# Both halves of eight FFN chunks as seven block products, with half of the down-projection between their steps

## Chip, cores, metric

One NeuronCore of a Trainium2 chip. The metric is the device time of one execution in microseconds.

## What is computed

A trunk of two decoder layers over 512 tokens of width 1024. Layer 0 mixes tokens by dilated attention, layer 1 by a gated linear recurrence (RG-LRU); after each mixer comes the same gated ConvFFN, which is where the change lies. Every sub-layer stands between two RMS norms, and the second norm's output is added to the residual stream.

```python
D_MODEL, SEQ, D_FF, FFN_CONV_WIDTH = 1024, 512, 3 * 1024, 3

def conv_ffn(x, w_up, conv_w, conv_b, w_down):       # w_up (1024, 6144), w_down (3072, 1024)
    u = causal_dwconv(x @ w_up, conv_w, conv_b)      # depthwise, 3 taps along the tokens
    g, v = u[..., :D_FF], u[..., D_FF:]
    return (jax.nn.gelu(g, approximate=True) * v) @ w_down
...
for layer in range(DEPTH):                           # 2 layers
...
    h = rms_norm(x, norm_ffn_pre[layer])
    h = conv_ffn(h, ffn_w_up[layer], ffn_conv_w[layer], ffn_conv_b[layer], ffn_w_down[layer])
    x = x + rms_norm(h, norm_ffn_post[layer])
```

All inputs are float32.

## The kernel before

**Numbers.** Every operand of a matmul is split into a high and a low part: `split` copies the raw values to fp32r on ACT (line 147), and VectorE subtracts that copy from the raw values (line 148). A product takes three matmuls (`PASSES`: high x high, high x low, low x high). Weights go through the same split, so each weight tile that TensorE uses costs one ACT copy and one VectorE subtraction of 128 x 512.

**Weights.** All weight loads stand in one list, `plan`, in the order of use. `load` fetches the next raw chunk (1 MB) on SP's queue into one of three buffers; `pump` converts the next piece of a chunk into one of 16 pairs of high and low buffers (`HALVES`, counted in `state["live"]`). `done` gives buffers back, `take` returns a converted piece. `tick` is called after each unit of TensorE's work and lets pending side work (`sides`) and the pump run, so conversions are issued some units ahead of their use. Every engine works through its instructions in the order in which the program gives them out.

**The FFN.** `hT` holds the normed tokens transposed, features on the partitions. The 3072 gelu features and the 3072 value features are cut into 12 chunks of 256 each, and a chunk into two tiles of 128 features by 512 tokens. A plain tile is 8 x 3 matmuls of 512 columns into one PSUM bank (`feat_tile`, or in four parts `quarters`). `begin` then does the convolution (line 749 on ACT, line 753 twice on VectorE) and returns the gelu (line 765, ACT) or the multiplication of gelu and value (the gate, line 767, VectorE).

For chunks 3 to 10 (`SEVEN`) the gelu half is made by a scheme of seven block products: the 256 features, the 1024 inputs and the 512 tokens are each cut in two, and seven products of combined blocks replace eight. The token-side sums come from `token_sums`, which runs as side work while the plain chunks 1 and 2 are computed and, before the change, goes on into the stage. The weight-side sums are made in the raw buffer by `stream`: VectorE additions (lines 198 and 202), and accumulating loads issued by POOL (`add_rows`, line 184), which add a block of the same weights from DRAM to the block that lies there. A step of a product is 12 matmuls of 256 columns (line 934).

`seven` writes out the order by hand as slots. Each period of `CYCLE` = 15 slots has the seven steps of one gelu chunk (`AT` gives their slots; step 4 falls into the next period) and eight quarters of plain value tiles as fillers (6 matmuls of 512 columns each, line 392). What must follow a step is registered with `later`, which gives it out a slot later. In the stage, one piece is pumped after each slot.

After the stage come what is left of chunk 10, chunk 11 and the down-projection (`rows_proj`, `rows_run`): 24 rows of 128 features, each with 1024 output columns in two halves, summed in eight PSUM banks (`acc`), two for each of the four tiles of 128 tokens. `act_split` splits the gated activations one row at a time. The order of passes finishes token tile 0 first, then 1, 2 and 3, so that `norms` of a tile (post-norm, residual, pre-norm and transposes for the next layer) run beside the matmuls of the next. Tile 0 is turned by VectorE and a trip through DRAM, tiles 1 to 3 by TensorE (line 482). `root_table` loads ACT's table for square roots.

The attention already has block products of a second form, `chain` (line 1160 on, matmuls on line 1173), whose two result banks are put together by two VectorE additions (lines 1186 and 1191) and three ACT copies, and whose steps stand at `QUAD`.

Of the kernel before, what the change touches and what calls it, by code (L numbers as in the profile page):

```python
# [11 lines left out]
F32 = mybir.dt.float32  # L12
# [27 lines left out]
AT = {5: 0, 1: 3, 3: 4, 2: 8, 6: 9, 7: 14, 4: 20}  # L40
CYCLE = 15
# [3 lines left out]
HALF = ("s1", "w11", "w12", "a22", "s2", "s3", "s4")  # L45
# [36 lines left out]
def kernel(  # L82
# [69 lines left out]
    raws, units, pieces = {}, {}, []  # L152
    sides, first_w, first_y, one = [], [], [], []

    def parts_of(kind, raw):
# [3 lines left out]
        if kind == "value":  # L159
            return [raw[:, 2 * i : 2 * i + 2, :] for i in range(2)]  # L160
# [28 lines left out]

    def stream(i0, n):  # L190

        items = []
        for c in range(n):
            i = i0 + 2 * c
# [5 lines left out]
            def upper(i=i):  # L200
# [4 lines left out]
            def value(m, i=i + 1):  # L205
                raw = lambda: parts_of("feat", raws[i])[m]
                return (i, m), lambda: [raw()[:, :4], raw()[:, 4:]], m == 1

            for at, item in (
                (-6, (None, lambda i=i: ahead(i))), (0, ("s1", "s1")), (0.1, (None, across)), (1, ("w12", "w12")),  # L210
                (2, ("w11", "w11")), (2.1, (None, upper)), (3, value(0)), (5, ("a22", "a22")), (7, ("s4", "w12")),
                (8, ("s2", "s1")), (11, ("s3", "w11")), (12, value(1)),
            ):
                if c or at >= 0:
                    if isinstance(item[0], str):
                        item = ((i, item[0]), lambda i=i, h=item[1]: [blocks(i)[h]], item[0] == "s3")
                    items.append((CYCLE * c + at, item))
# [43 lines left out]
    def refill():  # L261
# [8 lines left out]
        if plan[i][0] == "seven":  # L270
            n = 1
            while plan[i + 2 * n][0] == "seven":
                n += 1
            pieces.extend(stream(i, n))
            state["cv"] += 2 * n
        else:
# [4 lines left out]
            state["cv"] += 1  # L281

    def pump(limit=2):

        for _ in range(limit):
# [6 lines left out]
            if state["live"] + 2 - (pieces[0][0][1] in HALF) <= HALVES:  # L292
# [451 lines left out]
    def ffn(layer, hT, post, pre):  # L744
        ca, cc = ffn_cols[layer]

        def conv(ps, j):
            u = gen(s="u")
            nc.scalar.activation(  # L749
                u, ps, AF.Identity, scale=cc[:, j : j + 1], bias=cc[:, 48 + j : 49 + j]  # L750
            )
            for d, wc in ((1, ca[:, 48 + j : 49 + j]), (2, ca[:, j : j + 1])):
# [887 lines left out]
```

## Time and profile before

| | |
|---|---|
| median of the runs | 1431.78 us (2 runs, both 1431.78) |
| profiled execution | 1431.89 us, span 1430.1 us from first to last instruction |
| TensorE (PE) | busy 1420.4 us, 99% of the span, 8021 matmuls |
| weight loads (PEld) | 1246.0 us, 87% |
| VectorE (DVE) | 1022.3 us, 71% |
| ScalarE (ACT) | 723.2 us, 51% |
| GpSimd (POOL) | 176.2 us, 12% |
| granted TensorE clock, mean | 0.999 |
| DMA | 191.30 MB, mean 134 GB/s |

A matmul's busy time includes its fill and drain and so overlaps the next one's; what a run of matmuls costs is read from the chain in order of time. VectorE's instructions overlap a little too. An engine's idle time matters only where the chain passes through it. The first FFN's block-product stage lies from about 552 to 723 us of the span, the second's from about 1097 to 1269.

### The profile page before, as it was taken

The numbers are of one execution on the slowest core, as the hardware profiler recorded it, in microseconds if no ns is written. First come the engines' busy times: TensorE is split into PE (matmuls) and PEld (weight loads), VectorE is DVE, ScalarE is ACT, GpSimd is POOL, SyncE is SP. The second block draws the span as 40 slices with busy tenths as digits, with TensorE's granted clock in tenths as the row PEclk, the third lists the DMA queues.
The fourth block names the chain that finished last, engine by engine and source line by source line (L and its number), as shares of the span: only waits on it lengthen the run. The fifth ranks groups of instructions, "written<-read, shape, count | busy, mean of one in ns | idle before, by whom it ended". The sixth has DMA issues, their size and how long they took to land.

```text
span 1430.1 us, 21591 instructions
## 1 busy us (share of the span) xinstructions
PE 1420.4 (99%) x8021; PEld 1246.0 (87%) x8021; DVE 1022.3 (71%) x2017; ACT 723.2 (51%) x1486; POOL 176.2 (12%) x309
## 2 busy tenths in 40 slices
PE   9999999999999999999999999999999999999998
PEld 7888999999998888998988889888898999988886
DVE  6676898787855989877763348779789977764333
ACT  7343555363636555555553335588455555553321
POOL 0341333130400101110000001000101101000000
PEclk9999999999999999999999999999999999999999
DMA  7643455565756355554443222432335555443201
GB/s 225 181 146 106 131 166 156 166 184 138 195 166 221 113 184 118 119 147 134 139 163 118 88 74 90 134 116 89 117 111 151 145 118 118 141 178 116 88 1 59
DMA packets 143266, 191.30 MB, mean 134 GB/s; under 512 B 9344, under 2 KB 119384, under 8 KB 142648
## 3 DMA queue, kind: packets, MB, share of 16 engines
q1 hardware_dynamic: 114856, 147.57, 32.2%
q0 software_dynamic: 27456, 41.29, 12.7%
q8 instruction: 63, 1.03, 0.3%
q10 hardware_dynamic: 848, 1.05, 0.2%
q14 instruction: 43, 0.35, 0.1%
HBM read 170.93 MB, written 18.96 MB: 133 GB/s over the span
## 4 chain that ended last, share of the span: by engine, by line
PE 91%; ACT 4%; DVE 4%; DMA 1%; issue 1%; POOL 0%; DVEq 0%; SPq 0%; ACTq 0%
PE ps L392 32%; PE acc L392 24%; PE ps L934 11%; PE ps L1173 10%; PE v L1107 7%; PE v L1045 1%; DVE xb L1443 1%; DVE wlo L148 1%; PE O L1350 1%; PE S L1284 1%; PE S L1232 1%; ACT whi L147 1%; ACT sig L1464 1%; PE tr L482 1%; PE O L392 0%
## 5 line engine op out<-in xcount | busy, mean ns | idle before, releaser
L148 DVE TENSOR_TENSOR wlo<-raw,whi 128x512 fp32r<-128x512 f32 x600 | 395.5, 686 | 203.1 <-ACT whi L147 202.7
L147 ACT ACTIVATE whi<-raw 128x512 fp32r<-128x512 f32 x600 | 358.7, 627 | 301.6 <-PE acc L392 118.2
L392 PE MATMUL ps<-hT,whi 128*128 128x512 f32 (+1 forms) x1728 | 486.0, 367 | 0.0
L392 PEld LDWEIGHTS ps<-hT,whi 128*128 128x128 f32 x1728 | 308.2, 189 | 48.8
L392 PE MATMUL ps<-hT,wlo 128*128 128x512 f32 (+1 forms) x864 | 316.0, 366 | 0.0
L392 PE MATMUL acc<-whi,ahi 128*128 128x512 f32 x512 | 199.5, 390 | 0.0
L392 PE MATMUL acc<-whi,alo 128*128 128x512 f32 x512 | 199.3, 389 | 0.1
L392 PE MATMUL acc<-wlo,ahi 128*128 128x512 f32 x512 | 199.2, 389 | 0.0
L392 PEld LDWEIGHTS ps<-hT,wlo 128*128 128x128 f32 x864 | 162.9, 189 | 27.0
L753 DVE SCALAR_TENSOR_TENSOR u<-ps,cols,u 128x511 f32<-128x511 f32 x192 | 143.6, 748 | 48.9 <-ACT u L749 45.5
L749 ACT ACTIVATE u<-ps,cols 128x512 f32<-128x512 f32 x96 | 73.9, 770 | 82.3 <-DVE ps L949 41.7
L392 PEld LDWEIGHTS acc<-whi,alo 128*128 128x128 f32 x512 | 96.1, 188 | 20.6 <-DVE alo L148 0.5
L392 PEld LDWEIGHTS acc<-whi,ahi 128*128 128x128 f32 x512 | 96.1, 188 | 19.9
L392 PEld LDWEIGHTS acc<-wlo,ahi 128*128 128x128 f32 x512 | 96.1, 188 | 19.6
L1107 PE MATMUL v<-whi,hT 128*128 128x512 f32 x320 | 106.6, 396 | 0.0
L1173 PE MATMUL ps<-T,whi 128*128 128x256 f32 x512 | 93.7, 282 | 0.8 <-DVE ps L1191 0.8
L934 PE MATMUL ps<-T,whi 128*128 128x256 f32 x512 | 92.8, 280 | 0.0
L184 POOL DMA_DIRECT2D raw<-in_ffn_w_up_dram x32 | 41.5, 1442 | 362.1 <-DVE wlo L148 260.5
L1173 PEld LDWEIGHTS ps<-T,whi 128*128 128x128 f32 x512 | 79.7, 189 | 2.3 <-DVE ps L1191 1.2
L934 PEld LDWEIGHTS ps<-T,whi 128*128 128x128 f32 x512 | 80.1, 189 | 1.6
L443 POOL DMA_DIRECT2D ft<-turned x136 | 74.5, 555 | 28.9 <-issue 7.9
L1173 PE MATMUL ps<-T,wlo 128*128 128x256 f32 x256 | 72.0, 281 | 0.0
(211 smaller groups left out, 2008.5 us busy)
## 6 DMA issues: line engine op xcount, KB each, us to landing
raw<-in_ffn_w_up_dram SPq DMA_DIRECT2D x48, 1024.0 KB
raw<-in_attn_w_qkv_dram SPq DMA_DIRECT2D x67, 512.0 KB
raw<-in_ffn_w_down_dram SPq DMA_DIRECT2D x24, 1024.0 KB
raw<-in_ffn_w_up_dram POOLq DMA_DIRECT2D x32, 256.0 KB, 4.9
raw<-in_lru_w_in_dram SPq DMA_DIRECT2D x8, 1024.0 KB
turned<-T POOLq DMA_DIRECT2D x26, 256.0 KB, 2.6
ft<-turned POOLq DMA_DIRECT2D x104, 64.0 KB, 4.6
vrows<-v SPq DMA_DIRECT2D x16, 256.0 KB
```

The costliest lines, as they stand in the source:

```text
L147: nc.scalar.activation(hi, raw, AF.Copy)
L148: nc.vector.tensor_tensor(lo, raw, hi.bitcast(F32), op=ALU.subtract)
L184: nc.gpsimd.dma_start(to, src, accum_op=ALU.add)
L392: mm(dst, l[a], r[b], start=start and n == 0, stop=stop and n == 2)
L443: nc.gpsimd.dma_start(t[32 * c : 32 * c + 32].rearrange("j (b x) -> j b x", b=4), d.rearrange("(b j) (c x) -> c j b x", j=32, c=4)[c],)
L482: nc.tensor.transpose(ps[:, k * P : (k + 1) * P], xs[i][:, k * P : (k + 1) * P], ident)
L749: nc.scalar.activation(u, ps, AF.Identity, scale=cc[:, j : j + 1], bias=cc[:, 48 + j : 49 + j])
L753: nc.vector.scalar_tensor_tensor(u[:, d:], ps[:, : S - d], wc, u[:, d:], op0=ALU.mult, op1=ALU.add)
L934: mm(y[b][:, 0:256], W[wa][0][:, k, :], right[n](ha, k), start=n in (1, 5) and k == q == 0, stop=k == 3 and q == 2, skip_group_check=True,)
L1045: mm(banks[t], hT[a][:, k, t * P : (t + 1) * P], W[b][k % 2][:, 0, :], start=u == n == 0, stop=u == 3 and n == 5,)
L1107: mm(bank, hT[a][:, k, t * P : (t + 1) * P], W[b][k % 2][:, 0, :], start=(k, a, b) == (0, 0, 0), stop=(k, a, b) == (KD - 1, 1, 0),)
L1173: mm(dst, W[wa][0][:, k, :], right[n](ha, k), start=n in (1, 5) and k == q == 0, stop=k == 3 and q == 2, skip_group_check=True,)
```

## The change

- The value half of chunks 3 to 10 is made by block products as well, and both halves use `chain`, which is taken out of the attention and shared. Its second result is the negative of what is wanted, and `conv` uses negated taps for it (`neg`).
- A chain now has a period of 10 slots: seven steps and three free slots. The free slots take the four quarters of chunk 2's last value tile, as before, then the four plain tiles of chunk 11 (`up`), and then rows 0 to 15 of the down-projection's first column half: each row is two slots of two token tiles. Their weights come in their own small loads (`gen_load`) into general buffers.
- After the stage, `down` does rows 16 to 23 of the first column half, then all 24 rows of the second. The activations are split once for each half. `TAIL` and the order of passes finish the token tiles one after the other.
- `token_sums` in the FFN does its later parts without the pauses of eight and three ticks, puts the last block into weight buffers, and changes two signs.

```diff
-AT = {5: 0, 1: 3, 3: 4, 2: 8, 6: 9, 7: 14, 4: 20}
-CYCLE = 15
+LAST, FIRST, TAIL = 11, 16, 14
+AT = {1: 0, 5: 1, 2: 3, 6: 4, 3: 5, 7: 8, 4: 12}
+CYCLE, FREE = 10, (6, 7, 9)
+EARLY = 16
...
+    def free_slots(n):
+        end = CYCLE * n
+        free = [AT[4] - CYCLE] + [CYCLE * c + r for c in range(n) for r in FREE] + [end, end + 1, end + 3]
...
     def stream(i0, n):
...
             def across(i=i):
                 x = blocks(i)
                 nc.vector.tensor_tensor(x["s1"], x["s1"], x["w11"], op=ALU.add)
+                add_rows(x["w11"], plan[i][3][0][0][:, 0:4, P:256])
+            def lower(i=i):
+                x = blocks(i)
                 nc.vector.tensor_tensor(x["w12"], x["w12"], x["s1"], op=ALU.add)
-                add_rows(x["w11"], plan[i][3][0][0][:, 0:4, P:256])
...
+            if c:
+                items.append((o - 5, (None, lambda i=i: ahead(i))))
             for at, item in (
+                (-3, ("w11", "w11")), (0, ("s1", "s1")), (0.1, (None, across)), (1, ("w12", "w12")),
+                (3, ("s2", "s1")), (3.1, (None, lower)), (7.5, ("s4", "w12")), (8, ("s3", "w11")), (10.5, ("a22", "a22")),
...
+        for key, loads, cuts, length in direct:
+            u = free[at]
+            if loads:
+                items.append((u - EARLY, (None, loads)))
+            items.append((u - 1, ((i0, key), cuts, False)))
+            at += length
...
     def ffn(layer, hT, post, pre):
         ca, cc = ffn_cols[layer]
+        neg = cp.tile([P, 144], F32, tag="neg", name=nm("neg"))
+        nc.vector.tensor_scalar(neg[:, 0:96], ca, -1.0, None, op0=ALU.mult)
+        nc.vector.tensor_scalar(neg[:, 96:144], cc[:, 0:48], -1.0, None, op0=ALU.mult)
...
+        for k in range(FIRST):
+            w = ffn_w_down[layer][k * P : (k + 1) * P, 0:512].rearrange("(k p) c -> p k c", p=P)
+            o, load = gen_load(w)
+            direct.append((("rows", k), load, lambda o=o: [o[0]], 0))
+            direct.append((("act", k), None, lambda k=k: [act(k)], 2))
...
-        i = seven(hT, T, begin, i)
+        acc = seven(hT, T, begin, i)
         x_back()
-        prep(3)
-        for j in range(SEVEN[-1] + 1, 12):
-            tiles(j, i if j == SEVEN[-1] + 1 else chunk(), (1,) if j == SEVEN[-1] + 1 else (0, 1))
-            tiles(j, chunk(), (2, 3))
-        return run()
+        return down(acc, act, post, pre)
+
+    def down(acc, act, post, pre):
+        post_g = gain(*post)
+        pre_g, hT = (gain(*pre), new_hT()) if pre is not None else (None, None)
+        root_table()
+        n, four = 2 * 12, [0, 1, 2, 3]
+        passes = [(0, four, range(FIRST, n)), (1, four, range(TAIL))]
+        passes += [(1, [0], range(TAIL, n)), (1, [1], range(TAIL, n)), (1, [2, 3], range(TAIL, TAIL + 4))]
+        passes += [(1, [t], range(TAIL + 4, n)) for t in (2, 3)]
...
+        for n, (half, tiles, k) in enumerate(todo):
+            at = seq.index((half, k))
+            prep(at + 3)
+            W = take(ids[at // 4], at % 4 // 2)
+            for t in tiles:
+                ...
+                mm3(second[t] if half else acc[t], [a[:, t * P : (t + 1) * P] for a in A[half, k]], ...)
+                if half and k == 23:
+                    side(norms(t, [acc[t], second[t]], post_g, pre_g, hT))
...
+    def chain(right, top, bottom):
+        def step(n):
+            W = take(i, LEFT[n][0])
+            b, at = {1: (1, 0), 6: (1, 0), 7: (1, 0), 4: (1, 0), 5: (0, 256), 3: (0, 256), 2: (0, 0)}[n]
+...             
+            if n in (1, 5, 6):
+                later(1, lambda: nc.scalar.activation(to, dst, AF.Copy))
+            elif n == 3:
+                def upper():
+                    nc.vector.tensor_tensor(y[0], y[0], t[0], op=ALU.add)
+                    top(y[0])
+                later(1, upper)
+            elif n == 7:
+                later(1, lambda: nc.vector.tensor_tensor(y[1][:, 256:512], dst, t[1][:, 0:256], op=ALU.add))
+            elif n == 4:
+                later(1, lambda: bottom(y[1]))
...
     def seven(hT, T, begin, before):
...
+        def rows(k, pair):
+            W, A = take(i0, ("rows", k)), take(i0, ("act", k))
+            for t in pair:
+                if t not in acc:
+                    acc[t] = psum("acc")
+                mm3(acc[t], [a[0][:, t * P : (t + 1) * P] for a in A], [w[0] for w in W], not k, False)
...
+        for j in SEVEN:
+            for half in range(2):
+                f = chain(right, *ends(j, half))
+                steps.update((CYCLE * n + AT[p], f(p)) for p in AT)
+                n += 1
...
-        for j in range(12):
+        for j in range(LAST):
             for half in range(2):
-                w_cols(ffn_w_up[layer], half * D_FF + j * 256, kind="seven" if j in SEVEN and not half else "feat")
-        for c in range(12):
-            w_rows(ffn_w_down[layer], c * 256)
+                w_cols(ffn_w_up[layer], half * D_FF + j * 256, kind="seven" if j in SEVEN else "feat")
+        for half in range(2):
+            for k in range(0 if half else FIRST, 24, 4):
+                rows = ffn_w_down[layer][k * P : (k + 4) * P, half * 512 : half * 512 + 512]
+                plan.append(("value", 4, 512, [(rows.rearrange("(k p) c -> p k c", p=P), 512)]))
```

More of the change, by code (lines that the diff above doesn't have):

```diff
@@ L958, in fillers @@
-        def fillers(i, m, j, b):
-            return quarters(i, m, hT, lambda ps: finish(b, ps, j))
-        steps = {}
-        fill = fillers(before, 1, SEVEN[0] - 1, 3)
-        for n, j in enumerate(SEVEN):
-            f = chain(j, 0)
-            steps.update((CYCLE * n + AT[p], f(p)) for p in AT)
-            i = chunk()
-            steps.update((CYCLE * n + m, q) for m, q in zip((1, 2, 6, 7, 10, 11, 12, 13), fill + fillers(i, 0, j, 2)))
-            fill = fillers(i, 1, j, 3)
+        i0, acc = state["next"], {}
@@ L969, in seven @@
+        free = free_slots(n)
+        assert len(free) == len(fill)
+        steps.update(zip(free, fill))
         state["even"] = True
-        after = chunk()
-        end = CYCLE * len(SEVEN)
-        steps[end + 3] = steps.pop(max(steps))
-        fill += fillers(after, 0, SEVEN[-1] + 1, 0)
         for m in range(max(steps) + 1):
-            if m in steps or m >= end:
-                slot(steps[m] if m in steps else fill.pop(0))
-        for f in fill:
-            slot(f)
+            slot(steps[m])
```

257 lines of the change are left out of this document (130 added, 127 removed).

## The prediction

> **What bounds the kernel now.** I read the page's engine shares first, then its chain of waits by line.
>
> ```profile
> PE 1420.4 (99%) x8021; PEld 1246.0 (87%) x8021; DVE 1022.3 (71%) x2017; ACT 723.2 (51%) x1486; POOL 176.2 (12%) x309
> PE 91%; ACT 4%; DVE 4%; DMA 1%; issue 1%; POOL 0%; DVEq 0%; SPq 0%; ACTq 0%
> ```
>
> TensorE is the bound, nearly everywhere, so matmuls taken away are time taken away as long as nothing else starts to end last. The busy time of a matmul overlaps its neighbour's, so prices come from the chain in order of time (start, length, matmuls): one period of the block-product stage, both ends of the first FFN's down-projection, and the second FFN's whole.
>
> ```profile
> 593.88 2.75 PE ps L392 x12
> 596.62 4.31 PE ps L934 x36
> 600.93 2.75 PE ps L392 x12
> 603.68 2.85 PE ps L934 x24
> 606.53 5.47 PE ps L392 x24
> 612.01 2.80 PE ps L934 x24
> 872.76 5.46 PE acc L392 x24
> 878.21 5.75 PE ps L392 x48
> 1292.66 130.57 PE acc L392 x576
> ```
>
> In one period the 84 half-width matmuls (L934, 256 columns) take 4.31 + 2.85 + 2.80 = 9.96 us, 0.1186 each; the 48 full-width ones (L392) 2.75 + 2.75 + 5.47 = 10.97, 0.2285 each. Left alone in a down-projection a full-width one takes 130.57 / 576 = 0.2267. A slot of the schedule is 12 half-width or 6 full-width matmuls: 1.42 or 1.37 us.
>
> The windows (PE, PEld, DVE, ACT, POOL busy, clock, DMA share, GB/s) show how much room the others have: a period of this stage, a stretch of the attention where block products of the form that the change adopts run four abreast, and the end after the last matmul.
>
> ```profile
> 614.81:635.74 20.93, 20.93 (x133) 18.98 (x133) 16.15 (x26) 11.46 (x21) 2.59 (x2) 1.00 0.51 125
> 307.04:335.57 28.53, 28.53 (x242) 28.53 (x242) 23.12 (x39) 15.23 (x30) 9.82 (x18) 1.00 1.03 289
> 1424.00:1430.10 6.10, 0.00 (x0) 0.00 (x0) 2.60 (x7) 0.27 (x1) 0.00 (x0) 0.77 0.23 86
> ```
>
> VectorE is second: 77% of a period here, 81% in the attention's stretch, where TensorE did not stop.
>
> **The matmuls.** Sixteen value chunks (eight per FFN) go from 8 filler slots to 7 steps: 16 x (10.97 - 9.96) = -16.2 us. The fillers become 32 slots of down-projection and 20 of feature tiles. These matmuls exist today, but in unbroken runs; among half-width ones they cost 0.2285 instead of about 0.227: 624 x 0.0017 = +1.1. Together **-15.1 us**.
>
> **VectorE inside the new period.** Ten slots (7 x 1.42 + 3 x 1.37) make 14.1 us. The groups of the stage, the two adds of the attention's chain, and the distance of starts in the timeline:
>
> ```profile
> L148 DVE TENSOR_TENSOR wlo<-raw,whi 128x512 fp32r<-128x512 f32 x78 | 52.7, 687 | 21.2 <-ACT whi L147 21.2
> L753 DVE SCALAR_TENSOR_TENSOR u<-ps,cols,u 128x511 f32<-128x511 f32 x29 | 21.7, 749 | 11.3 <-ACT u L749 11.3
> L749 ACT ACTIVATE u<-ps,cols 128x512 f32<-128x512 f32 x28 | 21.5, 768 | 18.5 <-DVE ps L949 17.7 <-PE ps L392 0.5 <-PE ps L934 0.3
> L1186 DVE TENSOR_TENSOR ps<-ps,part 128x512 f32<-128x512 f32 x16 | 11.1, 691 | 0.0
> L1191 DVE TENSOR_TENSOR ps<-ps,part 128x256 f32<-128x256 f32 x16 | 6.8, 428 | 0.2 <-PE ps L1173 0.2
> 309.52 0.68 DVE L241 TENSOR_TENSOR raw<-raw 128x512 f32<-128x512 f32 x1
> 310.13 0.69 DVE L1186 TENSOR_TENSOR ps<-ps,part 128x512 f32<-128x512 f32 x1
> 310.85 0.69 DVE L1030 SCALAR_TENSOR_TENSOR qk<-ps,roots 128x512 f32<-128x512 f32 x1
> 630.20 1.54 DVE L753 SCALAR_TENSOR_TENSOR u<-ps,cols,u 128x511 f32<-128x511 f32 x2 [0.85 <-ACT u L749]
> 631.65 1.28 DVE L148 TENSOR_TENSOR wlo<-raw,whi 128x512 fp32r<-128x512 f32 x2
> ```
>
> A full tile lasts 0.69 but the next starts 0.60 later; a convolution pair takes 1.45. Per chain: 7 weight splits 4.2, two block sums 1.2, adds 0.72 and 0.43, two convolutions 2.9, a gate on average 0.6, and 1.5 rows with a weight and an activation split each 1.8: 11.9 us, and 0.85 of idling where a convolution waits for ACT behind an add. So 12.7 of 14.1: fuller than now, still under. ACT has 10 copies, 3 half copies, 2 convolutions and a gelu, about 9.5 of 14.1. The wider activation splitting (48 more over both FFNs) is in this sum or, in the down-projection, 1.2 of 2.7 us a row. The pump gives one piece a slot and a period uses ten in ten slots; followed through the code, every split comes 9 to 25 slots ahead of its use although two of the 16 buffers now hold block sums. So weights cost nothing; without that lead each late split would show in full (0.63 + 0.69).
>
> **DMAs.** Each chain sends two accumulating loads through POOL, 32 more in all:
>
> ```profile
> raw<-in_ffn_w_up_dram POOLq DMA_DIRECT2D x32, 256.0 KB, 4.9
> L184 POOL DMA_DIRECT2D raw<-in_ffn_w_up_dram x11 | 14.2, 1463 | 103.7 <-DVE wlo L148 103.7
> ```
>
> Issue 1.5 and landing 4.9 make 6.4 us; the block sum is split six slots (8.4 us) later, and nine further slots cover a delay. On SP the same bytes go in smaller loads (54 instead of 36 per FFN, the small ones 13 or more slots early); a period moves some 2.0 MB, 139 GB/s beside the 125 above. POOL's restore of x and the gains still queue behind the last block product and are wanted some 60 us later. I take 0.
>
> **A wait added inside a chain.** Step 4 overwrites the half bank that step 7's result is read from, four slots later (before: six). VectorE's add stands behind an upper half's convolution and several splits in its queue; step 4 holds back all of TensorE. The same four slots stand in the attention:
>
> ```profile
> PE ps L1173 <- DVE ps L1191: 0.8, 1, 0.8
> ```
>
> Once in 16 chains, 0.8 us. For 32 chains I take two such waits, **+1.6**; bounds 0 and 32 x 0.8 = 25.6.
>
> Where they would fall: the block sums of hT (token_sums) move forward. Parts three and four, eight VectorE instructions and four ACT copies per FFN, leave the stage, where they were spread over eight and three slots, and join the plain chunks 1 and 2:
>
> ```profile
> 510.90:551.80 40.90, 40.90 (x194) 34.37 (x193) 37.59 (x59) 20.80 (x35) 4.52 (x4) 1.00 0.52 148
> ```
>
> There VectorE already works 37.6 of 40.9 us; 8 x 0.6 = 4.8 more leave it some 1.5 us behind when the stage begins. TensorE doesn't see that in the plain chunks (eight PSUM banks of 5.5 us each lie between it and a late convolution); the first step 4 of each FFN, 12 slots on, is the first that could. The moved parts themselves are read by steps 7 and 4 at slots 8 and 12, over 11 us after they are issued. So I price the move inside the two waits, and at 2 us per FFN if the lag is not made up. The two small sign tables per FFN (neg) lie behind the norms: 0.
>
> **The start of the down-projection.** Before, three activation splits were prepared (prep(3)) ahead of chunk 11. Now they are issued after the last slot, behind whatever ACT has queued. How ACT spends that today (timeline; the table load then lies beside running matmuls):
>
> ```profile
> 733.75 1.66 ACT L147 ACTIVATE ahi<-u 128x512 fp32r<-128x512 f32 x3
> 747.48 1.14 ACT L147 ACTIVATE whi<-raw 128x512 fp32r<-128x512 f32 x2
> 748.64 1.28 ACT L414 ACT_TABLE_LOAD   x1
> 749.93 0.20 ACT L414 ACTIVATE s<-ident 128x1 f32<-128x1 f32 x1
> ```
>
> By the buffer count the last pump takes the two buffers that the stage's last matmuls release. So from that end: 1.14 of weight splits, 1.28 + 0.20 for the root table, 0.6 for the first activation copy, and about 0.25 of hand-over and of the low part: 3.5 us in which TensorE has nothing. Two FFNs: **+7.0**. Bounds: 1.3 each if those weight splits don't stand there, 4.2 if VectorE's convolution, splits and gate end last.
>
> The Trainium skill, "TensorE: Matmul & The Clock Gate", in its section on what is actually happening, says that an idle window of about 3.4 us halves the clock; the window runs freely. Above, the clock averages 0.77 over 6.1 idle us, so it fell some 3.3 us into that window, about 4 after the last matmul. By that rule a gap of 3.5 could hold a window, and the sum would be some 3 us more; by the row it just escapes.
>
> **Between the first FFN and the next layer.** After a row tile's last matmul come ACT's squares, VectorE's norm, and for tile 0 a turn through DRAM:
>
> ```profile
> 852.88 0.60 ACT L399 ACTIVATE junk<-acc 128x512 f32<-128x512 f32 x1 [0.67 <-PE acc L392]
> 869.98 0.63 ACT L475 ACTIVATE hT<-ft 128x512 fp32r<-128x512 f32 x1 [1.80 <-DMA ft<-turned]
> 874.20 0.68 DVE L555 TENSOR_TENSOR post<-acc,gain 128x512 f32<-128x512 f32 x1
> 886.29 0.88 DVE L465 TENSOR_SCALAR xs<-xs,s 128x512 f32<-128x512 f32 x2
> 887.54 1.04 PE L482 MATMUL tr<-ident,xs 128*128 128x128 f32 x8
> ```
>
> Tile 0's turn lands 17.1 us after its sums. The new tail leaves 90 matmuls and a transpose after tile 0: 21.2 us instead of 25.3. The landing then stands 4.1 us before the layer's end (878.21 today), ahead of ACT's copies of tile 1, and tile 2's norm starts about 2.3 us later relative to that end than today's 874.20. Tile 3's ends 11.3 after it instead of 9.0, and TensorE reaches its transposes 9.3 after: **+2.0**, bounds 0 and 4.
>
> **The end.**
>
> ```profile
> 1417.82 0.60 ACT L399 ACTIVATE junk<-acc 128x512 f32<-128x512 f32 x1 [0.67 <-PE acc L392]
> 1421.30 0.34 ACTq L562 DMA_DIRECT2D out_dram<-x_sb  x1
> ```
>
> The last tile has 18 matmuls (4.1 us) behind the one before instead of 24 (5.5). ACT is free of the former 3.8 us after its sums, then needs 0.8 for the first square: **+0.4**, bounds 0 and 0.7.
>
> **Sum.** -15.1 + 1.6 + 7.0 + 2.0 + 0.4 = -4.1. The profiled execution took 1431.89 (span 1430.1), 0.1 above the median shown; 1431.9 - 4.1 = **1427.8 us**.
>
> **Rivals.**
> - *All hidden*: the boundaries are covered and only the matmuls count, 1431.9 - 15.1 = 1416.8. For it: this stage runs today with TensorE never waiting. Against it: nothing is left for TensorE at the new boundary.
> - *Step 4 waits in every chain* (the other side). VectorE at 12.7 of 14.1 carries its backlog from chain to chain, and each step 4 waits 0.8: 1427.8 - 1.6 + 25.6 = 1451.8. It is slower than before from 0.18 us a chain (5.7 / 32). For it: 0.69 durations without overlap would make 13.1 + 0.85 of the 14.1, and the distance shrank from six slots to four. Against it: the attention's one wait in sixteen. "VectorE: DVE Perf Modes" in the Trainium skill, on the errata, exposes the memory latency between instructions, which speaks for the durations; the starts 0.60 apart disagree.
> - *The clock falls in each gap*: TensorE then runs at half speed for as long again as the gap (an estimate; no row shows the recovery), 1.75 lost twice: 1431.3. The gap is within about 0.5 us of where the end of this trace shows the fall.
>
> **How the numbers follow.** Forecast 0.5, all hidden 0.2, step 4 everywhere 0.2, clock 0.1. The range 1416.0 to 1442.0 takes in the first case and its bounds, the clock, and step 4's waits up to 0.5 us a chain; left out are the longer ones and what nothing above prices. A change of 2%, about what a measurement of this kernel tells from none, is 28.6 us: faster than 1403.1 needs nearly twice all the matmuls saved (0.01); slower than 1460.4 needs over 1 us at every step 4 (0.05); 0.94 lies between.
>
> **What would show it.** Right: steps and fillers in the windows at 14.1 us a chain with PE full and DVE at 84 to 90%; one hole of 3 to 4 us in PE before each first acc matmul of row 16, released by ACT's ahi, with a table load in it; about 2 us before the last transposes of the first FFN. Wrong: PE waits for DVE at the add in many chains, ACT waits for the accumulating loads, or no hole at the boundary.

## The result and the profile after

The changed kernel takes 1469.08 us (median of 2 runs, 1469.02 to 1469.14) against 1431.78: a ratio of 1.026, 95% interval 1.0216 to 1.0305. It is slower by 37.3 us where 4 less were forecast. The profiled execution has a span of 1467.1 us.

Three lines of the page answer to those shown of before: the engines, the chain that ended last, and the accumulating loads.

```profile
PE 1422.8 (97%) x8597; PEld 1271.6 (87%) x8597; DVE 1121.1 (76%) x2181; ACT 790.3 (54%) x1630; POOL 218.5 (15%) x341
PE 44%; DMA 6%; DVE 4%; issue 4%; ACT 2%; POOL 0%; DVEq 0%; ACTq 0%; POOLq 0%
raw<-in_ffn_w_up_dram POOLq DMA_DIRECT2D x64, 256.0 KB, 8.8
```

TensorE's waits (us in total, times, longest):

```profile
PE ps L1009 <- DVE ps L1027: 13.3, 8, 2.6
PE ps L1009 <- ACT part L1018: 10.8, 8, 3.1
PE acc L409 <- ACT ahi L149: 9.0, 2, 5.3
PE tr L499 <- DVE xs L482: 1.0, 1, 1.0
```

TensorE, which hardly waited before, stops 19 times: 8 times for VectorE's add of step 7's result, 8 times for ScalarE's copy of a partial result, twice at the start of the down-projection, once at the transition. An accumulating load lands after 8.8 us instead of 4.9. The windows (PE, PEld, DVE, ACT, POOL busy, clock, DMA share, GB/s) show where: stage start and boundary of the first FFN, the boundary of the second, and three undisturbed chains.

```profile
552.00:566.00 14.00, 10.90 (x72) 10.13 (x71) 11.70 (x19) 7.12 (x14) 2.58 (x2) 0.88 0.45 112
800.00:811.00 11.00, 5.71 (x15) 4.14 (x14) 7.05 (x11) 5.75 (x10) 0.00 (x0) 0.71 0.63 231
1365.00:1376.00 11.00, 7.29 (x21) 5.44 (x20) 7.54 (x12) 6.48 (x12) 0.00 (x0) 0.69 0.68 249
641.00:683.00 42.00, 42.00 (x305) 39.75 (x304) 37.31 (x59) 25.67 (x47) 5.17 (x4) 1.00 0.55 131
```

The undisturbed chains run as forecast, TensorE full and VectorE at 37.31 of 42 (89%). The time is lost at the two ends of each stage and in its first five chains.

*Stage start.* ScalarE's and VectorE's rows (timeline):

```profile
555.33 0.36 ACT L1018 ACTIVATE part<-ps 128x256 f32<-128x256 f32 x1
558.38 0.63 ACT L149 ACTIVATE whi<-raw 128x512 fp32r<-128x512 f32 x1 [2.69 <-DVE raw L207]
558.92 0.37 ACT L1018 ACTIVATE part<-ps 128x256 f32<-128x256 f32 x1
555.74 1.28 DVE L150 TENSOR_TENSOR T<-B,T 128x512 fp32r<-128x512 f32 x2
557.66 0.69 DVE L207 TENSOR_TENSOR raw<-raw 128x512 f32<-128x512 f32 x1
```

ScalarE stands 2.69 us before a weight split, because VectorE makes the block sum for it (L207) only after the moved token sums (T). The split is wanted by a later step. The copy of step 5's result queues behind it, and step 2, two slots after step 5, writes into that same bank. So TensorE stands 3.3 us from one matmul's start to the next (3.1 in the list of waits), and the granted clock averages 0.88 over these 14 us.

*First chains.* Pieces of the chain of waits, in order of time:

```profile
605.50 0.70 DVE raw L207
...
606.82 0.72 POOL raw L186
607.54 10.34 DMA raw<-in_ffn_w_up_dram
...
618.50 0.61 ACT u L785
619.12 0.27 ACT part L1018
619.39 0.53 ACT whi L149
619.92 0.05 issue
619.96 0.69 DVE wlo L150
620.65 0.62 DVE ps L1022
...
626.95 0.60 DVE raw L212
627.55 0.36 DVE ps L1027
627.90 0.04 issue
627.95 4.08 PE ps L1009 x32
```

An accumulating load takes 10.34 us. ScalarE stands before the split of its block until it lands (timeline):

```profile
617.97 0.63 ACT L149 ACTIVATE whi<-raw 128x512 fp32r<-128x512 f32 x1 [5.20 <-DMA raw<-in_ffn_w_up_dram]
```

So the copy that step 7 needs (619.12) is late and TensorE stops; then VectorE, fed late by the same queue, comes late with the add at L1027, and TensorE stops again at step 4. One late load, two stops.

*Boundary.* ScalarE's rows, and the matmuls after the hole:

```profile
802.55 1.15 ACT L149 ACTIVATE whi<-raw 128x512 fp32r<-128x512 f32 x2 [2.62 <-DMA raw<-in_ffn_w_down_dram]
803.71 1.28 ACT L431 ACT_TABLE_LOAD   x1
805.01 0.20 ACT L431 ACTIVATE s<-ident 128x1 f32<-128x1 f32 x1
805.12 1.65 ACT L149 ACTIVATE ahi<-u 128x512 fp32r<-128x512 f32 x3
805.78 0.79 PE L409 MATMUL acc<-whi,ahi 128*128 128x512 f32 x1 [5.29 <-ACT ahi L149]
806.38 0.63 PE L409 MATMUL acc<-wlo,ahi 128*128 128x512 f32 x1
806.80 0.63 PE L409 MATMUL acc<-whi,alo 128*128 128x512 f32 x1
```

These are the forecast's four pieces in the forecast's order, with 2.62 us of waiting for a raw load ahead of them. Then matmuls start 0.42 apart instead of 0.23; the granted clock is 0.50 from 805.7 to 811.0.

The time from each matmul's start to the next can be set against 0.1186 us for a half-width and 0.2267 for a full-width one. Summed over the span, the change brings 35.7 us more of stops (over 0.36 too long), 8.6 of stretches of 0.1 to 0.36 (in the main the low clock on full-width matmuls), and 6.4 of smaller ones: 50.7. At the same prices its matmuls take 14.7 us less, and 1.0 more lies behind the start of the last matmul (8.28 us instead of 7.28): -14.7 + 50.7 + 1.0 = +37.0, the whole difference of the spans. By place, the change loses 9.8 us at the two starts, 23.5 in the first chains behind them and 14.8 at the two boundaries.

### The profile page after: what moved, and what is told of

Read it like the earlier page. It is cut to its first block, busy times and chain, and to the rows that moved or that the text cites. A ratio compares the mean times of both kernels' runs of the same rounds, so it can differ in the third digit from the quotient of the medians.

```text
span 1467.1 us, 23340 instructions
## 1 busy us (share of the span) xinstructions
PE 1422.8 (97%) x8597; PEld 1271.6 (87%) x8597; DVE 1121.1 (76%) x2181; ACT 790.3 (54%) x1630; POOL 218.5 (15%) x341
## 4 chain that ended last, share of the span: by engine, by line
PE 44%; DMA 6%; DVE 4%; issue 4%; ACT 2%; POOL 0%; DVEq 0%; ACTq 0%; POOLq 0%
PE acc L409 17%; PE ps L1009 15%; PE ps L409 10%; DMA raw<-in_ffn_w_up_dram 4%; DMA raw<-in_ffn_w_down_dram 2%; PE gate L409 1%; DVE wlo L150 1%; ACT whi L149 1%; DVE u L772 0%; DVE x_sb L577 0%; DVE post L572 0%; ACT u L770 0%; DVE ps L1022 0%; PE tr L499 0%; POOL ft L460 0%
## 5 line engine op out<-in xcount | busy, mean ns | idle before, releaser
L409 PE MATMUL ps<-hT,whi 128*128 128x512 f32 (+1 forms) x1216 | 327.8, 357 | 0.0
L1009 PE MATMUL ps<-T,whi 128*128 128x256 f32 x1536 | 284.8, 285 | 17.7 <-DVE ps L1027 13.3
L1009 PEld LDWEIGHTS ps<-T,whi 128*128 128x128 f32 x1536 | 241.2, 191 | 24.9 <-DVE ps L1027 15.7
L409 PEld LDWEIGHTS ps<-hT,whi 128*128 128x128 f32 x1216 | 213.8, 189 | 30.3
L1009 PE MATMUL ps<-hT,whi 128*128 128x256 f32 x1152 | 215.5, 285 | 6.6 <-ACT part L1018 6.6
L1009 PE MATMUL ps<-T,wlo 128*128 128x256 f32 x768 | 216.3, 282 | 0.0
L409 PE MATMUL ps<-hT,wlo 128*128 128x512 f32 (+1 forms) x608 | 216.2, 356 | 0.0
L1009 PEld LDWEIGHTS ps<-hT,whi 128*128 128x128 f32 x1152 | 183.5, 193 | 11.2 <-ACT part L1018 7.9
L1009 PE MATMUL ps<-hT,wlo 128*128 128x256 f32 x576 | 163.9, 285 | 0.0
L1009 PEld LDWEIGHTS ps<-T,wlo 128*128 128x128 f32 x768 | 147.4, 192 | 0.0
L772 DVE SCALAR_TENSOR_TENSOR u<-ps,cols,u 128x511 f32<-128x511 f32 (+1 forms) x128 | 95.8, 748 | 37.0 <-ACT u L770 34.7
```

What stands on the lines that cost most here:

```text
L409: mm(dst, l[a], r[b], start=start and n == 0, stop=stop and n == 2)
L772: nc.vector.scalar_tensor_tensor(u[:, d:], ps[:, : S - d], wc, u[:, d:], op0=ALU.mult, op1=ALU.add)
L1009: mm(dst, W[wa][0][:, k, :], right[n](ha, k), start=n in (1, 5) and k == q == 0, stop=k == 3 and q == 2, skip_group_check=True,)
```

## The experiments

A time without an interval comes from one run; the kernel before took 1431.9 to 1433.4 beside these. "Waits" are TensorE's for the partial results in the stages (adds at step 4 + copies; 13.3 + 10.8 in the change).

**The boundary.** `e4_prep_early` gives out the table load and the first three activation splits after slot 160, three slots ahead of the stage's end.

```diff
             slot(steps[m])
+            if m == 160:
+                early()      # root_table(); split rows 16 to 18
...
-        root_table()         # in down()
```

> The root table and the first three activation splits of the down-projection are given out after slot 160 of the stage, three slots before its end, instead of after it. Theory H (the hole before the down-projection is ACT's queue: late weight splits, table load, copy): the holes of 5.6 and 4.0 us go and with them the 13 and 12 matmuls at a lowered clock, 4.9 and 4.2 us: 1469 - 18.7 = about 1450 us. Rival W (TensorE lacks weights there, whose 1 MB load lands 13.8 us after issue): the hole shrinks to the wait for that load, 2.6 us or more, and about 1460 us.

Measured: 1451.98, near theory H. Both holes and the low clock after them are gone; of the waits in the stages most stay (10.9 + 9.4). By the starts of the matmuls, 14.6 of the 17.1 us gained lie at the boundaries (8.3 + 6.5 in the change, 0.1 + 0.1 here), the rest in the first chains. The boundary needs nothing but an earlier place in ScalarE's queue.

**The stage start.** `e3_sums_light` leaves out the third and fourth token block sums, and steps 7 and 4 read the first and second instead.

```diff
-        T.extend([homes[2 * n], homes[2 * n + 1]] for n in range(4))
+        T.extend([homes[2 * n], homes[2 * n + 1]] for n in (range(4) if first else (0, 1, 0, 1)))
+        if not first:
+            return
```

> Leaves out the third and fourth block sum of the tokens in both FFNs (8 VectorE instructions and 4 ACT copies each): steps 7 and 4 read the first and second sum in their place, so the FFN's values differ; the matmuls are as many as before. Theory B (VectorE enters the stage behind because of the moved sums, and ACT stands behind it when step 5's result is to be copied): the first gap of the stage, 3.4 us in each FFN, goes, and the lowered clock behind it: 1469 - 6.8 - 2 = about 1460 us. Rival (the gap comes from the first accumulating load or the weight sums, not from the token sums): it stays, 1469 us.

Measured: 1450.53, 18.5 us less where 9 were expected. Waits for copies fall from 10.8 to 1.3 us and the start's stop from 3.3 to 0.6: with this order of steps the moved sums are what makes the start late. The waits for adds stay (14.2). That the boundaries shrink to 5.1 from 9.0 was not foreseen, and its cause was not traced. `e7_late_sums` keeps them, on top of the early preparation, and gives out the last quarter three slots later.

```diff
         parted(2, b12)
-        yield 1 + first
+        yield 2 if first else 4
```

> The kernel of the early preparation (1452.0) with one thing more: the last quarter of the token-side sums (four VectorE adds, two splits) is given out three slots later, inside the stage, as step 4 needs it only at slot 12. Theory (VectorE is behind when the stage begins because these sums were put into the plain chunks, and the stage's first steps wait for that): the 3.3 us at each start shrink to about 1, with the lower clock after them, 8 to 10 us in all: 1442 to 1444. Rival (the start waits for the first chain's own weight sums, the later sums only trade places with them): 1450 or more.

Measured: 1446.04, 6 us less than 1451.98 where 8 to 10 were expected. The start's stop falls from 3.3 to 0.6, and the clock stays up:

```profile
552.00:566.00 14.00, 13.54 (x94) 12.31 (x93) 12.15 (x20) 7.66 (x15) 2.59 (x2) 1.00 0.69 149
```

But a stop of 2.8 us appears in the next chain, where `e4` had none: the lag moves on in part.

**The loads.** `e2_raw_later` gives the 1 MB raw loads out 6.5 slots later in the list, to part them from the accumulating loads; `e6_ahead` gives the accumulating load out 8 instead of 5 slots early (with the early preparation), and `e8_ahead_late` does that together with the late sums.

```diff
+            items.append((o + (17 if c < n - 3 else 10.6), (None, fetch)))    # e2: load() from the list
...
-                items.append((o - 5, (None, lambda i=i: ahead(i))))
+                items.append((o - 8, (None, lambda i=i: ahead(i))))           # e6, e8
```

> Same work as the changed kernel, but each 1 MB raw weight load of the stage is given out 6.5 slots (about 9 us) later in the order, away from the two accumulating loads, instead of right behind the split that frees its buffer. Theory L with collision (the accumulating loads land late because they share the DMA engines with the 1 MB load issued in the same microsecond): they land in 4.6 to 6.9 us, ACT's waits for them go, about 1450 us. Rival L without collision (they are late because two stand in POOL's queue behind a wait for ACT and VectorE): landings stay near 9 us, time within 5 us of 1469. Rival V: no change.

> The kernel of the early preparation (1452.0) with one thing more: the first accumulating load of each block sum is given out 8 slots ahead of the split that needs it instead of 5 (11.3 us instead of 7). Theory (the load lands 8 to 11 us after its issue, so five slots are too few, and ScalarE, which takes its work in order, stands before that split): the gaps of 0.5 to 2.6 us inside the first chains go, about 7 us in each FFN, while the 3.3 us at the stage's start stay: 1437 to 1441. Rival (the load waits for bandwidth that the raw loads and the small loads take at that time, and lands when they are through, however early it is issued): 1449 or more.

> Both edits of the two kernels before on top of the early preparation. If the gaps at the start and those inside the first chains have the two separate causes: the gains add, 1426 to 1434, at or below the kernel before the change. If one gap only shows what another hides (work that comes late waits at the next place): 1437 or more.

Measured: 1461.44, 1450.75 and 1446.42. Against 1451.98 and 1446.04 `e6` gains 1.2 and `e8` loses 0.4: nothing, as the rivals said. `e2` fits none of its forecasts: its landings stay near 9 us (8.4), yet it gains 8. But none of the three changed what it meant to. SP's first raw load of the stage in the timeline of the change:

```profile
558.98 0.37 SPq L334 DMA_DIRECT2D raw<-in_ffn_w_up_dram  x1
```

The same of `e2_raw_later`:

```profile
558.79 0.37 SPq L342 DMA_DIRECT2D raw<-in_ffn_w_up_dram  x1
```

Here the load starts at the same time although its instruction stands 6.5 slots later; the likely reason is that it waits for its buffer. POOL, too, works ahead of the slots: it sends the next chain's accumulating load right behind this chain's (from 559.13 on in `e4`, from 558.66 in `e6`, where the instruction stands three slots earlier). So these runs hardly speak on the collision. Why `e2` is 8 us faster than the change was not traced.

`e10_raw_pool` (early preparation, late sums) puts the raw loads into POOL's own queue, where the order does hold.

```diff
+            eng = nc.gpsimd if kind == "seven" and i and plan[i - 1][0] == "seven" else nc.sync
-            nc.sync.dma_start(raw[...], src)
+            eng.dma_start(raw[...], src)
```

> The kernel with the early preparation and the late last quarter of the token sums (1446.0), with one thing more: the 1 MB raw loads of the stage go into POOL's queue, behind the accumulating loads, instead of SP's. In the trace of the change both start at the same moment (558.88 and 558.98) and the accumulating loads land after 9 to 11 us, against 4.6 before the change. Theory (two queues share the DMA engines, so the accumulating loads are stretched by the raw loads beside them, and ScalarE's queue stands until they land): landings back to 4.5 to 7 us, the gaps inside the first chains (2.8, 1.2, 2.0, 2.5, 1.1 and the like in the second FFN, some 19 us together) down to about 4: 1428 to 1433. Rival (the stretch comes from the small loads or from the landings' own pace, or VectorE ends last anyway): landings still 8 or more, or gaps as before: 1443 or more. If POOL's longer issue of 1 MB loads holds the next accumulating load back: gaps later in the stage, over 1450.

Measured: 1457.38, slower than 1446.04. The theory held for the load that stands ahead of the raw load, but the other came behind it. DMA issues from 555 to 575 us (of the three accumulating loads, two stand ahead of a raw load and land in 4.9 and 4.6, one behind it takes 10.3):

```profile
raw<-in_ffn_w_up_dram POOLq DMA_DIRECT2D x2, 1024.0 KB, 9.0
raw<-in_ffn_w_up_dram POOLq DMA_DIRECT2D x3, 256.0 KB, 4.9
```

The waits grew to 21.1 + 4.6. So the raw load beside it is what stretches an accumulating load: the small loads run on in all these kernels, and the change itself has a pair (588.34) whose raw load starts 3 us later and which lands in 4.6 and 6.7. Parting only one of the two does not help.

`e1_dve_sums` does all block sums with VectorE, without any accumulating load; `e9_dve_late` does so with the early preparation and the late sums.

```diff
+                (-2.9, (None, first)),       # VectorE: s1 += a22, for ahead(i)
-                add_rows(x["w11"], plan[i][3][0][0][:, 0:4, P:256])
+                nc.vector.tensor_tensor(x["w11"], x["s1"], x["a22"], op=ALU.subtract)   # in lower()
```

> The block sums of the weights in the FFN stages are made by VectorE alone (two more additions of 128x512 per chain, as the attention does it), so POOL sends no accumulating loads there. Theory L (ACT stands before a split whose accumulating load has not landed, 9 to 11 us after issue, and the copies that TensorE's steps need stand behind it): the seven waits after the stage's start go, 10.5 us in the first FFN and 9.5 in the second, with some 2 us of lowered clock: about 1447 us. Rival V (VectorE is simply too full at 12.7 of 14.1 us a chain and the late additions are its backlog): 1.2 us more per chain make it fuller, the waits at the addition grow and spread to later chains: 1475 us or more.

> Early preparation, block sums by VectorE alone (no accumulating load), and the last quarter of the token-side sums three slots later. If accumulating loads and the late VectorE at the start are all that is left: close to the sum of matmuls, 1420 to 1428. If VectorE, which then carries 13.9 of 14.1 us in a period, ends last: 1440 or more, with waits of TensorE for VectorE's adds in many chains.

Measured: 1456.42, between L's 1447 and V's 1475, and 1444.25, as if VectorE ended last. Without any accumulating load `e9` still waits 13.4 us for the adds at step 4 (+2.4 for copies). The loads were one way to be late; with 64 more sums of 0.6 us VectorE is late without them. Neither theory alone was right: step 4's four slots are too few in both cases.

**The distances between steps.** `e17_step4_alone` changes the kernel of the change in one thing: step 4 stands at slot 16 instead of 12, eight slots behind step 7, and its weight split moves along, which frees the raw buffer some 4 us later.

```diff
-CYCLE, FREE = 10, (6, 7, 9)
+CYCLE, FREE = 10, (2, 7, 9)
+    def at_slot(c, n, p):
+        return 16 if p == 4 and c < n - 1 else AT[p]
...
-                ... (10.5, ("a22", "a22")),
+                ... (14.5 if c < n - 1 else 10.5, ("a22", "a22")),
```

> The kernel of the change with step 4 at slot 16 alone, its weight split with it (the raw loads then start about 5 us after the accumulating ones). Theory (the step-4 distance and the collision of the loads make the gaps inside the first chains, some 20 us in both FFNs; the starts, 2 x 6, and the boundaries, 2 x 7 with the low clock, stay): 1449 to 1456. Rival (the chains' gaps come with the starts' backlog and move on to other steps): 1462 or more.

Measured: 1450.20, 19 us less. The waits at step 4 are all but gone (1.3 us). What is left are copies: 10.3. The accumulating loads land in 4.7, and the raw load starts 3.7 us behind them (timeline):

```profile
559.27 2.59 POOL L186 DMA_DIRECT2D raw<-in_ffn_w_up_dram  x2 [19.13 <-issue]
562.99 0.37 SPq L337 DMA_DIRECT2D raw<-in_ffn_w_up_dram  x1
```

So two things changed at once, the distance and the landing; this run doesn't part them.

The same move with other mends: `e12_step4_dve` on `e9`, `e13_step4_acc` on `e7`, and `e14_step4_ahead` as `e13` with the raw loads in POOL's queue behind both accumulating ones (`o - 9.8`).

> The kernel with VectorE's block sums, early preparation and late token sums (1444.3) with one thing more: step 4 of each chain but the last stands at slot 16 instead of 12 (it trades places with a free slot), so eight slots instead of four lie between step 7 and the step that overwrites its half bank; its weight split moves with it. Theory (what is left, 2.9, 1.7, 1.0 and 0.7 us in each FFN, are waits of step 4 for VectorE's add of step 7's result, which stands behind a backlog): those waits go, some 12 to 15 us with the lower clock after them: 1428 to 1432. Rival (VectorE, at 13.9 of 14.1 us, is the bound, and its lag shows at the next place, a split that comes late): 1440 or more.

> The same move of step 4 with the accumulating loads kept (early preparation, late token sums; 1446.0 without the move). The later split of the last block also releases the raw buffer about 5 us later, so that the 1 MB load no longer starts together with the accumulating loads. Theory: both the waits at step 4 and ScalarE's stands before the loads go: 1420 to 1428, faster than before the change. Rival (late splits show at steps 6 and 7 instead): 1438 or more.

> As the kernel before, and the raw loads stand in POOL's queue behind both accumulating loads, whose order is accumulating, accumulating, raw (in the trial of POOL's queue it was accumulating, raw, accumulating, and only the first landed in 4.6 us; the second took 6.4 to 10.9). Theory: both accumulating loads land in under 7.5 us everywhere; if the later raw release of the kernel before already separates them, the two kernels agree within 2 us; if not, this one is faster by 3 us or more. If POOL's queue makes the raw loads late: slower by 5 or more.

Measured: 1454.84, 1437.17, 1433.26. In `e12`, which has no accumulating loads, the distance alone takes the waits for adds to 0.9; but those for copies rise from 2.4 to 23.1: with VectorE that full the lag only moves (the rival). `e13` misses its 1420 to 1428, since the copies stay: it keeps 0.8 + 10.1, `e14` 0.9 + 9.4 (landings 4.8 and 5.6). Timed again in five rounds (`e19_step4_ahead_again`), `e14` takes 1434.72, ratio 1.0024 (1.0014 to 1.0033). Its nine runs lie between 1433.64 and 1437.80, so `e13` isn't shown to differ from it.

> The best kernel so far, timed in rounds: 1433 again, within 0.2% of the kernel before the change.

The waits left stand before step 2. `e15_swap` puts step 2 a slot later and step 6 a slot earlier, `e16_swap_spread` also spreads the last token sums further.

```diff
-AT = {1: 0, 5: 1, 2: 3, 6: 4, 3: 5, 7: 8, 4: 12}
+AT = {1: 0, 5: 1, 6: 3, 2: 4, 3: 5, 7: 8, 4: 12}
```

> The best kernel so far (step 4 at slot 16, raw loads behind the accumulating ones, early preparation, late token sums; 1433.3) with steps 2 and 6 of each chain changing places (slots 4 and 3), their weight splits too. Step 2 writes into the bank from which ScalarE copies step 5's result, and now has three slots instead of two behind it. Theory (the 0.7, 2.3, 1.8 and 0.6 us that are left in each FFN are waits for that copy, held up in ScalarE's queue): each gap shrinks by up to a slot, 1.4 us, about 7 to 8 us in all: 1425 to 1427. Rival (step 6, now earlier, waits in the same way for the copy of step 1, or for its block sum): 1431 or more.

> The same with the last quarter of the token sums spread over five further slots (step 4 needs it only at slot 16 now). Theory (the 2.3 us gap in the second chain comes from VectorE's backlog of these sums): 1 to 3 us below the kernel before. Rival (it comes from the block sum's own place in the queue): the same within 0.5 us.

Measured: 1440.74 and 1440.51, slower than `e14`: the rival. TensorE now waits for copies 16 times instead of 8, in the later chains before step 6. ScalarE in `e15`, where TensorE goes on at 764.3:

```profile
762.85 0.63 ACT L149 ACTIVATE whi<-raw 128x512 fp32r<-128x512 f32 x1 [1.90 <-DVE raw L210]
763.38 0.61 ACT L149 ACTIVATE whi<-dw 128x512 fp32r<-128x512 f32 x1
763.90 0.36 ACT L1030 ACTIVATE part<-ps 128x256 f32<-128x256 f32 x1
```

The split that was moved forward now stands directly behind VectorE's block sum (L210), and step 1's copy behind that split. Spreading the token sums further changed nothing.

`e18_spaced` gives every such pair at least three slots, with all the mends of `e14`; `e20_spaced_alone` has this order of steps and nothing else on the kernel of the change.

```diff
+AT = {1: 0, 5: 1, 2: 4, 6: 5, 3: 7, 7: 9, 4: 13}        # step 4 at 16 but in the last chain
+CYCLE, FREE = 10, (2, 3, 8)
```

> The best kernel so far (step 4 at slot 16, raw loads behind the accumulating ones, early preparation, late token sums; 1433.3) with the steps spaced so that every step that writes into a bank from which a copy is read comes at least three slots after the copied one: 1 at 0, 5 at 1, 2 at 4, 6 at 5, 4 at 16, 3 at 7, 7 at 9; free slots 2, 3, 8. Swapping steps 2 and 6 alone made it slower, since step 6 then stood three slots behind step 1 but still within two of step 5's copy. Theory (the copies are only held up in ScalarE's queue): the 0.7, 2.3, 1.8, 0.6 us in each FFN shrink to 1 to 2 in all: 1424 to 1428, faster than before the change. Rival (VectorE's lag sets the pace there): 1432 or more.

> The kernel of the change (1469) with nothing but the spaced order of steps of the fastest kernel: 1 at 0, 5 at 1, 2 at 4, 6 at 5, 4 at 16, 3 at 7, 7 at 9, the free slots at 2, 3, 8, and the last split with step 4. Token sums, boundary and queues as in the change. Theory (the distances inside a chain were too short for ScalarE's in-order queue; the late loads and the VectorE backlog only show through them): the starts and the chains lose nearly all, some 5 us stay there, and the boundaries' 2 x 6 to 7: 1430 to 1436. Rival (the starts' 3.3 us come from VectorE's backlog however the steps stand): 1437 to 1446.

Measured: `e18_spaced` 1422.76 us (five rounds), ratio 0.9938 (0.9925 to 0.9952): 8.8 us faster than the kernel before. `e20_spaced_alone` 1436.94 (three rounds), ratio 1.0038 (1.0026 to 1.0051). TensorE's waits in `e20`:

```profile
PE acc L412 <- ACT ahi L149: 6.1, 2, 3.1
PE ps L1012 <- ACT part L1021: 4.1, 3, 1.7
PE acc L412 <- DVE alo L150: 1.2, 2, 0.7
PE ps L1012 <- DVE ps L1030: 1.0, 1, 1.0
```

Its accumulating loads on the page:

```profile
raw<-in_ffn_w_up_dram POOLq DMA_DIRECT2D x64, 256.0 KB, 4.8
```

TensorE's waits in `e18`:

```profile
PE ps L1021 <- ACT part L1030: 2.3, 2, 1.2
PE ps L1021 <- DVE ps L1039: 1.0, 1, 1.0
```

`e18` does a little better than its theory, `e20` a little worse (1436 at most was expected): a stop of 1.9 us stays at each start. The order of the steps, with the last split that moves along, takes back 32 of the 37 us; the instructions are the same, only their slots differ. Against `e17`, where the accumulating loads land as fast (4.7), the waits for copies fall from 10.3 to 4.1, so here the distances do it without the landing. Most of what remains over `e18` lies at the boundaries: 11.6 of 14.2 us by the starts of the matmuls.

## Why the prediction was wrong

**Right.** The matmuls: three undisturbed chains run at the forecast pace with TensorE full and VectorE at 89% (forecast 84 to 90%). The order and contents of the hole at the boundary. The transition: 1.0 us for the 2.0 taken, within its bounds. The end was small but took 1.0 for 0.4, beyond its bound of 0.7. Two signs that the forecast had named for being wrong came: TensorE waiting for the add, and ScalarE for the accumulating loads.

**Wrong: "every split comes 9 to 25 slots ahead of its use ... So weights cost nothing", and for the DMAs "nine further slots cover a delay ... I take 0".** The splits were indeed early enough for the steps that read them: the list of waits has none of TensorE for a weight in the stages. The step failed because it asked only who reads the split. ScalarE takes its work in order, and a split that waits for its block sum, slots ahead of need, holds up the copies behind it, which are wanted within two to four slots. The same holds for VectorE's adds. The forecast asked what stands ahead of the add for step 4, but not what stands ahead of the copies. The landing time, carried over as 4.9, was 8.8 at the median, since in the change's order of splits the raw buffer comes free just as the accumulating loads are sent (558.98 and 558.88). With that the first chains lost 23.5 us, where 1.6 was in the sum.

**Mis-sized: the four slots of step 4, at +1.6.** The waits at step 4 measured 13.3 us, inside the bounds of 0 to 25.6. But the two slots between steps 5 and 2, and the four between 6 and 7, were given no price; the waits for copies took 10.8. The attention's single wait of 0.8 was no measure, likely because its queues hold other work between the same steps; no run tests that.

**Wrong: the move of the token sums, priced "inside the two waits, and at 2 us per FFN if the lag is not made up".** "TensorE doesn't see that in the plain chunks ... the first step 4 of each FFN ... is the first that could" named the wrong step: step 2, nine slots sooner, saw it, for 3.3 us in each FFN and a lower clock after it, 9.8 us at the two starts.

**Mis-sized: the start of the down-projection, 7.0.** The waits measured 9.0 in the change and 7.3 (6.1 + 1.2) in `e20`. The raw load has a part in that: the first splits stood 2.62 and 1.03 us for it in the change, 0.23 in the first FFN of `e20`. With the low clock behind the holes the boundaries cost 14.8, twice the forecast.

**The clock.** Over the 11 us around the two boundary holes the granted clock is 0.71 and 0.69, over the start 0.88; with the stop at 0.6 it stays at 1.00. The forecast set it as a rival at 0.1, because, by its one row, a gap of 3.5 "just escapes". It belonged into the sum. The rule that was weighed there, from the Trainium skill ("TensorE: Matmul & The Clock Gate", section What's actually happening: an idle window of about 3.4 us halves the clock), agrees with the longer holes, but shorter stops were enough here. The first row below holds a stop of 2.55 us of the change, the second one of 2.75:

```profile
590.00:596.00 6.00, 3.60 (x20) 3.40 (x19) 4.70 (x9) 2.14 (x6) 0.92 (x1) 0.76 1.07 199
625.00:631.00 6.00, 3.41 (x29) 3.21 (x28) 4.93 (x9) 3.52 (x8) 0.00 (x0) 1.00 1.06 189
```

In `e12` a stop of 2.0 us sufficed; its half-width matmuls start 0.21 us apart instead of 0.12 from 622.4 to 625.8:

```profile
619.00:625.00 6.00, 4.16 (x25) 4.01 (x25) 5.38 (x10) 3.09 (x7) 0.00 (x0) 0.78 0.20 51
```

In the FFNs and behind them, over all these runs, no stop of 1.0 to 1.95 us was followed by a lower clock within five us, every one of 3.4 or more was, and between the two it went either way.

**The rivals.** "Step 4 waits in every chain" came nearest in sign and place. Its mechanism was another: not a steady backlog of VectorE, since from the sixth chain on TensorE all but never waits (0.2 us in both FFNs), but a lag that starts with late sums and late loads in the first five and shows wherever the next distance is short.

**Open.** Why `e2` gained 8 us, and why `e3` shortened the boundaries. How the 19 us of `e17` divide between the distance and the landing. That step 2 waits for a copy from the other half of its bank is seen in the waits; whether the hardware needs it was not tried.

## What to carry to other kernels

When work is put closer together, list for each engine what stands in its queue ahead of the results that the bounding engine needs soon, not only whether each operand is ready in time: an early, unneeded piece that waits holds up a late, urgent one. A pair of steps that share a result bank needs a distance that covers the longest thing in that queue. Here two slots were too few for a copy and three (4 us) enough once nothing else was late; for the add behind VectorE four were too few and seven enough. A stop of TensorE is paid twice where the clock falls behind it: here always from 3.4 us on, and sometimes from 2.0.

## What the hardware showed beyond expectation

- Accumulating loads of 256 KB: a median of 4.9 us before, 8.8 (10.34 in the chain above) when 1 MB raw loads start beside them, 4.8 in `e20`, where the first raw load starts 3.7 us behind them.
- The place of a DMA in the program said little of its time: given out 6.5 slots later, the first raw load started at 558.79 instead of 558.98.
- After a hole of 5.3 us matmuls started 0.42 us apart instead of 0.23, for some 5 us. After a stop of 2.0 us the clock fell too, 1.4 us after the matmuls had gone on.
